# Ranking TensorE's uses of VectorE results forty places later in a two-block fp32 network on one core

## The chip, the cores and the metric

One core of a Trainium2 chip runs the whole program in one launch. The metric is device time in microseconds, from the first to the last instruction with what lies around them; lower is better.

## The reference

Two networks run one after the other on 256 tokens of width 1024, in fp32. The first has two layers: a normalised and modulated input goes through one wide projection, then through three kinds of heads, and back through `w_out`. The second has two layers on 256 latent and 256 context tokens: a projection, a convolution, a gated recurrence (mLSTM) in both directions, attention with grouped keys, three gated branches, and a convolutional feed-forward part.

```python
def _layer(x, c, ...):                       # block 1, twice
    h = _rmsnorm(x, norm_g) * (1.0 + scale) + shift
    rq, rk, rv, rg, xbc, dt_raw, z, fq, fk, fv, fg, f_raw = split(h @ w_in)
    ret = _retention(rq, rk, rv, positions) * silu(rg)
    ssd = _rmsnorm((_ssd(xs, dt, A, Bm, Cm) + d_skip * xs) * silu(z), ssd_norm_g)
    fox = _forgetting_attention(fq, fk, fv, log_f) * silu(fg)
    return x + gate * (concatenate([ret, ssd, fox]) @ w_out)

def token_mixers(hx, hc, ...):               # block 2, twice
    conv = conformer_conv(cu, ...)
    mlstm = mlstm_readout(mlstm_bidirectional(...), mo, ...)
    attn = latent_attention(q, k, v) @ w_attn_out
    return (g_conv * conv + g_mlstm * mlstm + g_attn * attn) @ w_out
```

## The kernel before, in words

Weights are streamed: `_fetch` (L486) loads a strip of up to 1024 columns, ScalarE rounds it to a high part `hi` and VectorE subtracts to get the low part `lo`. `mm3` (L529) makes each fp32 product of three matmuls (high by high, high by low, low by high), so a projection of eight row blocks is 24 matmuls, 256 columns wide (512 in block 2, layer 0, and wherever keys of both segments are made). These projections are most of TensorE's work.

Between them stand the heads. Each head is cut into pieces that wait in the queue `bg`; `strip` (L511), called by every projection, takes pieces off at a set rate before it loads its weights, and `pump` and `drain` take more by hand. A piece alternates between engines: TensorE makes scores, VectorE and ScalarE turn them into weights, TensorE transposes these (L1223, L1613) or multiplies with them (L1114, L1229, L1624). The lines that the diff touches, with what they write and read:

- L1114, `ssd_pair` (block 1): products of the decay weights `ssd_E`, into an `aux` bank.
- L1183, `ret_gate` (block 1): transpositions of the gated retention output `rope_o`.
- L1223 and L1229, `fox_pair` (block 1): transpositions of the softmax weights `ret_fox`, and products of these (`fox_pT`) with the values.
- L1521, `attn_keys` (block 2): transpositions of the rotated keys `kv`.
- L1582, `queries` (block 2): transpositions of the rotated queries `qraw`.
- L1613, in `pair`: transpositions of the scaled exponentials `tA`, of which there are two buffers; L1624, in `pv`: products of the transposed weights `pT` with the values, which become `ao`, the input of the branch projection `w_attn_out_2`.
- L1822, in `finish` (block 2): transpositions of a finished mLSTM head `h`, which become `mo`.

Other names that occur: L470, L475, L457 are helpers that issue VectorE operations, L479 issues ScalarE's; L506 is the subtraction of `_fetch`; L1671 and L1676 are the scans of the gate chain; L1101 broadcasts a row for `ssd_pair`; L1204 to L1207 make the scores of `fox_pair`, L1601 those of `pair`; L1749 and L1757 make an mLSTM head's scores and decays.

The order of the work: the program is written once, straight through, and a planner fixes the order of each engine's queue before the kernel runs. It goes through the program with its own estimates of durations; whenever an engine is free in that model, it takes, of the instructions whose inputs are ready there, the one of lowest rank. The rank is the place in the program, counted one for each instruction of any engine. `prio` (L450) adds to it for what is traced inside:

```python
    @contextmanager
    def prio(self, offset):
        self.tc.cur_priority += offset
        yield
        self.tc.cur_priority -= offset
```

Some work already uses it: the gate chain of block 2 has a rank 1000 later, background sums of the modulation 300 later. On the chip each engine then follows its queue in order, and waits where an input is late. PSUM has eight banks: three named `mm` for projections, three `aux` for heads' products, two `tr` for transpositions.

Of the kernel before, what the change touches and what calls it, by code (L numbers as in the profile page):

```python
# [18 lines left out]
P = 128  # L19
# [20 lines left out]
HAND = 320  # L40
HAND_TILES = 1
HOLD = 2

FILL_PARTS = (1, 3, 6, 9)
CTX_ROWS = (0, 4, 8, 9, 10, 11, 12, 13)
# [322 lines left out]
class Kern:  # L368
# [72 lines left out]
    def dumpx(self, name):  # L441
        if self.opts.get("dump") and name in self.opts["dump"]:
            d = self.nc.dram_tensor("dump_" + name, (P, KD, 512), F32, kind="ExternalOutput").ap()
            for k in range(KD):
                for sg in range(2):
                    if sg or self.xc:
                        self.nc.sync.dma_start(out=d[:, k, 256 * sg:256 * sg + 256], in_=self.x_view(sg)[k])

    @contextmanager
    def prio(self, offset):  # L450
# [642 lines left out]
    def ssd_pair(self, l, p, cbm, xs, xdt, yd):  # L1093
        nc = self.nc
        g = p // 4
        pr = self.ps("aux")
        prv = pr.rearrange("p (h t) -> p h t", h=2)
        E = self.bt([P, 2, 384], "ssd_E", bufs=2)
        for hh in range(2):
            h = 2 * p + hh  # L1100
            nc.tensor.matmul(prv[:, hh], self.sel(h), self.RHL, start=True, stop=True)  # L1101
            for t in range(2):
                self.ts(E[:, hh, 256 * t:256 * t + P], prv[:, hh, P * t:P * t + P], self.RT[:, t, h:h + 1], ALU.subtract,
                        0.0, ALU.min)
            self.act(E[:, hh, P:256], prv[:, hh, P:256], AF.Exp, bias=self.offb[:, h:h + 1])
        for t in range(2):
            dg = E[:, :, 256 * t:256 * t + P]
            self.act(dg, dg, AF.Exp)
        self.mul(E, E, cbm[:, g:g + 1].to_broadcast([P, 2, 384]))
        py = self.ps("aux")  # L1110
        for t, (o0, e0) in enumerate(((0, 0), (P, 256))):
            for hh in range(2):
                c0 = P * p + 64 * hh
                nc.tensor.matmul(py[64 * hh:64 * hh + 64, o0:256], xdt[:, t, c0:c0 + 64], E[:, hh, e0:e0 + 256 - o0],  # L1114
                                 start=t == 0, stop=t == 1)
        self.stt(yd[:, p], xs[:, p], self.v(f"dskip{l}", p), py[:, 0:256], ALU.mult, ALU.add)

# [51 lines left out]
    def ret_gate(self, pt, ro, rr, n, fl):  # L1169

        nc = self.nc
        gt = self.bt([P, 2, 256], "rope_o", bufs=2).rearrange("p t c -> p (t c)")
        self.act(gt, pt, AF.Tanh, scale=0.5)
        self.stt(gt, gt, 1.0, pt, ALU.add, ALU.mult)
        for t in range(2):
            for hh in range(2):
                h = 2 * n + hh
                g = gt[:, 256 * t + P * hh:256 * t + P * hh + P]
                self.stt(g, ro[:, t, P * h:P * h + P], rr[:, 4 * t + h:4 * t + h + 1], g, ALU.mult, ALU.mult)
        ptr = self.ps("tr")  # L1180
        for hh in range(2):
            for t in range(2):
                nc.tensor.transpose(ptr[:, 256 * hh + P * t:256 * hh + P * t + P],  # L1183
                                    gt[:, 256 * t + P * hh:256 * t + P * hh + P], self.ident)
        pv = ptr.rearrange("p (h t) -> p h t", h=2)
        hi, lo = fl[0][:, 2 * n:2 * n + 2], fl[1][:, 2 * n:2 * n + 2]
        self.act(hi, pv, AF.Copy, scale=0.5)
        self.stt(lo, pv, 0.5, hi.bitcast(F32), ALU.mult, ALU.subtract)

    def fox_pair(self, p, fq, fk, fv, fo):  # L1190

        nc = self.nc
        pT = self.bt([P, 2, 384], "fox_pT", bufs=2)
        for hh in range(2):
            h = 2 * p + hh
            q, k = fq[:, p, hh], fk[:, p]
            pl = self.ps("aux")
            one = self.id2[:, 32 + h:33 + h]

            e = self.bt([P, 384], "ret_fox", bufs=3)  # L1200
            for t in range(2):
                o = pl[:, P * t:P * t + P + P * t]
                w = P + P * t
                nc.tensor.matmul(o, q[:, P * t:P * t + P], k[:, 0:w], start=True, stop=False)  # L1204
                nc.tensor.matmul(o, self.nid2[:, 32 + h:33 + h].to_broadcast([P, P]), self.FHL[:, 0:w], start=False, stop=False)
                nc.tensor.matmul(o, self.FHL[:, P * t:P * t + P], one.to_broadcast([P, w]), start=False, stop=False)
                nc.tensor.matmul(o[:, P * t:], self.idr, self.fmask, start=False, stop=True)  # L1207
            sm = self.bt([P, 8], "fox_sm", bufs=2)
            for t in range(2):
                o = pl[:, P * t:P * t + P + P * t]  # L1210
                nc.vector.tensor_reduce(sm[:, t:t + 1], o, axis=AX.X, op=ALU.max)
            self.ts(sm[:, 2:4], sm[:, 0:2], -0.125, ALU.mult)
            for t in range(2):
                o = pl[:, P * t:P * t + P + P * t]
                self.act(e[:, P * t:P * t + P + P * t], o, AF.Exp, scale=0.125, bias=sm[:, 2 + t:3 + t], accum=sm[:, 4 + t:5 + t])
            nc.vector.reciprocal(sm[:, 6:8], sm[:, 4:6])
            for t in range(2):
                ev = e[:, P * t:P * t + P + P * t]
                self.act(ev, ev, AF.Copy, scale=sm[:, 6 + t:7 + t])
            ptr = self.ps("tr")  # L1220
            for b in range(3):

                nc.tensor.transpose(ptr[:, P * b:P * b + P], e[:, P * b:P * b + P], self.ident)  # L1223
            self.act(pT[:, hh], ptr[:, 0:384], AF.Copy)
        po = self.ps("aux")
        for t, (o0, e0) in enumerate(((0, 0), (P, 256))):
            for hh in range(2):
                c = slice(P * p + 64 * hh, P * p + 64 * hh + 64)
                nc.tensor.matmul(po[64 * hh:64 * hh + 64, o0:256], fv[:, t, c], pT[:, hh, e0:e0 + 256 - o0],  # L1229
                                 start=t == 0, stop=t == 1)  # L1230
        self.act(fo[:, p], po[:, 0:256], AF.Copy)

# [264 lines left out]
    def attn_keys(self, l, kvp):  # L1497

        nc = self.nc
        small = lambda n, nm: self.b2.tile([P, n], F32, tag=nm, name=f"{nm}{l}", bufs=1)  # L1500
        kv = self.s4([P, 4, 256], F32, "kv")
# [16 lines left out]
            self.rope(l, tab, kv[:, t, 0:P], t, 1, 2, r[:, 2 * t:2 * t + 2])  # L1518
        pt = self.ps("tr")
        for t in range(4):  # L1520
            nc.tensor.transpose(pt[:, P * t:P * t + P], kv[:, t, 0:P], self.ident)  # L1521

        kh, kl = [self.s4([P, 2, 512], FR, nm) for nm in ("kh", "kl")]
        for e in range(2):
# [48 lines left out]
    def attn_pieces(self, l, at, full, T0, T):  # L1573
        nc = self.nc
# [3 lines left out]
        def queries(p):  # L1578

            pt = self.ps("tr")  # L1580
            for i in range(T // P):
                nc.tensor.transpose(pt[:, P * i:P * i + P], at["q"][p // 2][:, i, P * (p % 2):P * (p % 2) + P], self.ident)  # L1582
            q = st["q"] = self.s4([P, 2, T], FR, "q")
            for e in range(2):
                src = pt[64 * e:64 * e + 64, :T]
                self.act(q[0:64, e], src, AF.Copy)
                self.sub(q[64:128, e], src, q[0:64, e].bitcast(F32))

        def pair(p, seg, t):
# [15 lines left out]
            exs = [self.t2(P * nk, "tA") for e in range(2)]  # L1605
# [3 lines left out]
            for e in range(2):  # L1609
                self.ts(exs[e], exs[e], sm[:, 6 + e:7 + e], ALU.mult)  # L1610
                pt = self.ps("tr")
                for j in range(nk):
                    nc.tensor.transpose(pt[:, P * j:P * j + P], exs[e][:, P * j:P * j + P], self.ident)  # L1613
                self.act(st["pT", e][:, :, P * t:P * t + P], pt[:, :P * nk].rearrange("p (j t) -> p j t", j=nk), AF.Copy)

        def pv(p, seg):
            nk = 2 if seg == 0 else 4
            q0 = 256 * seg - T0
            if len(at["out"]) == p:
                at["out"] += self.hl(1, "ao", T)  # L1620
            po = self.ps("aux")
            for j in range(nk):
                for e in range(2):
                    nc.tensor.matmul(po[64 * e:64 * e + 64, 0:256], at["v"][:, j, P + 64 * e:P + 64 * e + 64],  # L1624
                                     st["pT", e][:, j], start=j == 0, stop=j == nk - 1)
            hi, lo = at["out"][p]
            self.split(hi[:, q0:q0 + 256], lo[:, q0:q0 + 256], po[:, 0:256])
            at["left"] -= 1
# [96 lines left out]
    def head_pieces(self, l, hd, head, T0, T, mo):  # L1725
        nc = self.nc
        q, k = head["q"], head["k"]
# [84 lines left out]
        def finish():  # L1812
# [6 lines left out]
            for f in range(2):  # L1819
                pt = self.ps("tr")[:, :T]  # L1820
                for i in range(ni):
                    nc.tensor.transpose(pt[:, P * i:P * i + P], ho[:, i, P * f:P * f + P], self.ident)  # L1822
                (hi, lo), = self.hl(1, "mo", T)
                w = self.v(f"m_norm2{l}", 2 * hd + f)
                self.act(hi, pt, AF.Copy, scale=w)
# [187 lines left out]
```

## Time and profile before

| | |
|---|---|
| median of 3 runs | 2198.2 us (2197.14 to 2200.11) |
| profiled execution, its own time | 2200.12 us |
| its span | 2198.4 us |
| mean granted TensorE clock | 0.997 |
| busy: TensorE, weight loads, VectorE, ScalarE | 2146.0, 1910.5, 1714.4, 1000.6 us |
| instructions | 38207, of them 14481 matmuls |
| DMA | 330.71 MB, mean 150 GB/s |

PE is TensorE's matmuls, PEld its weight loads, DVE is VectorE, ACT ScalarE, POOL GpSimd, SP the engine that issues the loads. A row `PE tr L1613 <- DVE tA L470` tells that TensorE, about to write a `tr` bank from line 1613, stood idle until VectorE had written `tA` in line 470. An fp32 matmul outside `mm3` and outside a transposition is recorded as two matmuls. A matmul's end is modelled, and the next one often starts before it.

### The profile page before, as it was taken

What the parts mean: (1) busy time and instruction counts of PE and PEld (TensorE: products, weight loads), DVE (VectorE), ACT (ScalarE), POOL (GpSimd) and SP (SyncE); (2) the same over time, 40 slices, a digit from 0 to 9 for tenths busy, and PEclk for the clock granted to TensorE, in tenths of its full rate; (3) what the DMA queues carried; (4) which work ended last, traced back from release to release, by engine and by line L of the source; (5) the groups of instructions that cost most, each with busy time, mean ns of one, the idle gap of its engine ahead of it and who ended that gap; (6) DMA issues with size and microseconds to landing.
All of it is one profiled execution on the core that took longest, in us unless ns stands there. A gap on an engine that the chain in (4) does not pass through costs nothing. (4 is left out here: it accounts for less than half of the span.)

```text
span 2198.4 us, 38207 instructions
## 1 busy us (share of the span) xinstructions
PE 2146.0 (98%) x14481; PEld 1910.5 (87%) x14481; DVE 1714.4 (78%) x3551; ACT 1000.6 (46%) x1828; POOL 72.0 (3%) x657
## 2 busy tenths in 40 slices
PE   6999999999999999999999999999999999999999
PEld 5999989898877888888888888888887999999999
DVE  6986889798975999775476777766689977567877
ACT  4656555555455333432333443323355434445654
POOL 0000000001000000000000000000000000000000
PEclk9999999999999999999999999999999999999999
DMA  8665746567321144235443244453432453674665
GB/s 301 198 202 176 268 135 201 160 215 235 106 68 53 50 128 144 82 123 160 125 154 110 82 125 128 122 181 122 122 116 72 128 156 126 210 249 145 186 195 158
DMA packets 98264, 330.71 MB, mean 150 GB/s; under 512 B 10912, under 2 KB 14368, under 8 KB 97952
## 3 DMA queue, kind: packets, MB, share of 16 engines
q1 hardware_dynamic: 97632, 326.47, 47.0%
q8 instruction: 114, 1.87, 0.4%
q0 software_dynamic: 448, 1.81, 0.2%
q14 instruction: 70, 0.57, 0.1%
HBM read 325.08 MB, written 3.15 MB: 149 GB/s over the span
## 5 line engine op out<-in xcount | busy, mean ns | idle before, releaser
L479 ACT ACTIVATE hi<-raw 128x1024 fp32r<-128x1024 f32 (+3 forms) x494 | 492.0, 997 | 709.0 <-PE mm L534 440.0
L506 DVE TENSOR_TENSOR lo<-raw,hi 128x1024 fp32r<-128x1024 f32 (+3 forms) x494 | 565.0, 1144 | 231.0 <-ACT hi L479 228.3
L533 PE MATMUL mm<-h,hi 128*128 128x512 f32 (+1 forms) x1296 | 445.7, 345 | 3.4 <-ACT th L479 1.2
L535 PE MATMUL mm<-h,lo 128*128 128x512 f32 (+1 forms) x1296 | 442.0, 342 | 2.5 <-DVE lo L506 2.5
L534 PE MATMUL mm<-h,hi 128*128 128x512 f32 (+1 forms) x1296 | 442.1, 342 | 0.4 <-DVE h L475 0.4
L533 PEld LDWEIGHTS mm<-h,hi 128*128 128x128 f32 x1296 | 244.3, 189 | 33.7 <-ACT h L479 1.5
L535 PEld LDWEIGHTS mm<-h,lo 128*128 128x128 f32 x1296 | 244.8, 189 | 32.3 <-DVE lo L506 3.3
L534 PEld LDWEIGHTS mm<-h,hi 128*128 128x128 f32 x1296 | 244.7, 189 | 30.3 <-DVE h L475 0.8
L533 PE MATMUL mm<-hi,h 128*128 128x256 f32 x608 | 173.2, 285 | 0.8 <-ACT h L479 0.7
L534 PE MATMUL mm<-lo,h 128*128 128x256 f32 x608 | 171.8, 283 | 1.2 <-DVE lo L506 1.2
L535 PE MATMUL mm<-hi,h 128*128 128x256 f32 x608 | 172.2, 283 | 0.1
L533 PE MATMUL mm<-h_hi,hi 128*128 128x256 f32 x512 | 143.7, 282 | 4.0 <-ACT h_hi L479 2.3
L535 PE MATMUL mm<-h_hi,lo 128*128 128x256 f32 x512 | 143.4, 282 | 1.3 <-DVE lo L506 1.2
L534 PE MATMUL mm<-h_lo,hi 128*128 128x256 f32 x512 | 143.8, 282 | 0.7 <-DVE h_lo L457 0.5
L475 DVE SCALAR_TENSOR_TENSOR cv<-glu,vec,cv 128x512 f32<-128x512 f32 (+1 forms) x240 | 136.4, 615 | 2.5 <-ACT cv L479 2.4
L766 DVE SCALAR_TENSOR_TENSOR ada<-ada,cb 128x1024 f32<-128x1024 f32 x104 | 126.8, 1220 | 1.3 <-DMA ada<-aall 0.8
L533 PEld LDWEIGHTS mm<-hi,h 128*128 128x128 f32 x608 | 114.4, 188 | 2.7 <-ACT h L479 1.8
L534 PEld LDWEIGHTS mm<-lo,h 128*128 128x128 f32 x608 | 114.5, 188 | 2.1 <-DVE lo L506 1.4
L535 PEld LDWEIGHTS mm<-hi,h 128*128 128x128 f32 x608 | 114.6, 189 | 1.3 <-DVE h L475 0.9
L533 PEld LDWEIGHTS mm<-h_hi,hi 128*128 128x128 f32 x512 | 96.1, 188 | 5.1 <-ACT h_hi L479 2.7
L535 PEld LDWEIGHTS mm<-h_hi,lo 128*128 128x128 f32 x512 | 96.1, 188 | 2.1 <-DVE lo L506 1.9
L534 PEld LDWEIGHTS mm<-h_lo,hi 128*128 128x128 f32 x512 | 96.3, 188 | 1.6 <-DVE h_lo L457 1.1
(679 smaller groups left out, 4821.9 us busy)
## 6 DMA issues: line engine op xcount, KB each, us to landing
raw<-wall SPq DMA_DIRECT2D x400, 512.0 KB, 3.7
ada<-aall SPq DMA_DIRECT2D x120, 512.0 KB, 4.2
raw<-wall SPq DMA_DIRECT2D x32, 384.0 KB, 3.1
raw<-wall SPq DMA_DIRECT2D x32, 320.0 KB, 3.1
raw<-wall SPq DMA_DIRECT2D x32, 256.0 KB, 2.7
yd<-aall SPq DMA_DIRECT2D x2, 1024.0 KB, 10.3
qk_ret<-aall SPq DMA_DIRECT2D x2, 1024.0 KB, 11.3
xs<-aall SPq DMA_DIRECT2D x2, 1024.0 KB, 10.8
```

The lines of the kernel that those rows point to most:

```text
L475: return self.nc.vector.scalar_tensor_tensor(out=out, in0=a, scalar=s, in1=b, op0=op0, op1=op1)
L479: return self.nc.scalar.activation(out, a, f, bias=bias, scale=scale, **kw)
L506: self.last_lo = self.nc.vector.tensor_tensor(lo[:, :w], raw[:, :w], hi[:, :w].bitcast(F32), op=ALU.subtract)
L533: mm(ps, ah, bh, start=first and n == 0, stop=False)
L534: mm(ps, ah, bl, start=False, stop=False)
L535: self.last_mm = mm(ps, al, bh, start=False, stop=last and n == len(A) - 1)
L766: nc.vector.scalar_tensor_tensor(out=out, in0=raw, scalar=1.0, in1=self.cb[which][i], op0=ALU.mult, op1=ALU.mult, accum_out=m[:, n:n + 1])
```

## The change

Two helpers are added, `late_t` for a transposition and `late_mm` for a product; each traces its instruction with a rank 40 higher. Nine lines call them in place of the direct call. Nothing else changes: the instructions, their operands and their buffers are the same, and so are the ranks of all others.

```diff
+T_LATE = 40
...
+    def late_t(self, out, a):
+
+        with self.prio(T_LATE):
+            self.nc.tensor.transpose(out, a, self.ident)
+
+    def late_mm(self, *a, **kw):
+        with self.prio(T_LATE):
+            self.nc.tensor.matmul(*a, **kw)
...
@@ ssd_pair
-                nc.tensor.matmul(py[64 * hh:64 * hh + 64, o0:256], xdt[:, t, c0:c0 + 64], E[:, hh, e0:e0 + 256 - o0],
+                self.late_mm(py[64 * hh:64 * hh + 64, o0:256], xdt[:, t, c0:c0 + 64], E[:, hh, e0:e0 + 256 - o0],
                                  start=t == 0, stop=t == 1)
@@ ret_gate
-                nc.tensor.transpose(ptr[:, 256 * hh + P * t:256 * hh + P * t + P],
-                                    gt[:, 256 * t + P * hh:256 * t + P * hh + P], self.ident)
+                self.late_t(ptr[:, 256 * hh + P * t:256 * hh + P * t + P], gt[:, 256 * t + P * hh:256 * t + P * hh + P])
@@ fox_pair
-                nc.tensor.transpose(ptr[:, P * b:P * b + P], e[:, P * b:P * b + P], self.ident)
+                self.late_t(ptr[:, P * b:P * b + P], e[:, P * b:P * b + P])
...
-                nc.tensor.matmul(po[64 * hh:64 * hh + 64, o0:256], fv[:, t, c], pT[:, hh, e0:e0 + 256 - o0],
+                self.late_mm(po[64 * hh:64 * hh + 64, o0:256], fv[:, t, c], pT[:, hh, e0:e0 + 256 - o0],
                                  start=t == 0, stop=t == 1)
@@ attn_keys
-            nc.tensor.transpose(pt[:, P * t:P * t + P], kv[:, t, 0:P], self.ident)
+            self.late_t(pt[:, P * t:P * t + P], kv[:, t, 0:P])
@@ queries
-                nc.tensor.transpose(pt[:, P * i:P * i + P], at["q"][p // 2][:, i, P * (p % 2):P * (p % 2) + P], self.ident)
+                self.late_t(pt[:, P * i:P * i + P], at["q"][p // 2][:, i, P * (p % 2):P * (p % 2) + P])
@@ pair
-                    nc.tensor.transpose(pt[:, P * j:P * j + P], exs[e][:, P * j:P * j + P], self.ident)
+                    self.late_t(pt[:, P * j:P * j + P], exs[e][:, P * j:P * j + P])
@@ pv
-                    nc.tensor.matmul(po[64 * e:64 * e + 64, 0:256], at["v"][:, j, P + 64 * e:P + 64 * e + 64],
+                    self.late_mm(po[64 * e:64 * e + 64, 0:256], at["v"][:, j, P + 64 * e:P + 64 * e + 64],
                                      st["pT", e][:, j], start=j == 0, stop=j == nk - 1)
@@ finish
-                    nc.tensor.transpose(pt[:, P * i:P * i + P], ho[:, i, P * f:P * f + P], self.ident)
+                    self.late_t(pt[:, P * i:P * i + P], ho[:, i, P * f:P * f + P])
```

## Rows read from the trace of the kernel before

**Rows 1.** The page: busy time and share of an engine; TensorE's granted clock in 40 slices.

```profile
PE 2146.0 (98%) x14481; PEld 1910.5 (87%) x14481; DVE 1714.4 (78%) x3551; ACT 1000.6 (46%) x1828; POOL 72.0 (3%) x657
...
PEclk9999999999999999999999999999999999999999
```

**Rows 2.** Who TensorE waited for: total us, times, longest us.

```profile
PE tr L1613 <- DVE tA L470: 3.1, 4, 2.0
...
PE tr L1822 <- DVE h L475: 1.9, 3, 0.8
PE tr L1521 <- DVE kv L457: 1.8, 2, 1.0
...
PE tr L1223 <- ACT ret_fox L479: 0.9, 3, 0.5
...
PE aux L1114 <- DVE ssd_E L457: 0.6, 1, 0.6
...
PE tr L1183 <- DVE rope_o L475: 0.5, 1, 0.5
PE aux L1229 <- ACT fox_pT L479: 0.5, 2, 0.3
...
PE tr L1582 <- DVE qraw L457: 0.4, 1, 0.4
```

**Rows 3.** TensorE's timeline, block 2 layer 1: start us, us shown; idle time in brackets.

```profile
1857.58 0.28 PE L534 MATMUL mm<-h,hi 128*128 128x256 f32 x1
1857.70 0.28 PE L535 MATMUL mm<-h,lo 128*128 128x256 f32 x1
1858.81 0.44 PE L1822 MATMUL tr<-cst,h 128*128 128x128 f32 x2 [0.83 <-DVE h L475]
1859.01 0.36 PE L533 MATMUL mm<-h,hi 128*128 128x256 f32 x1
```

**Rows 4.** TensorE's timeline at the longest wait of L1613.

```profile
1680.93 1.06 PE L1613 MATMUL tr<-cst,tA 128*128 128x128 f32 x8 [1.96 <-DVE tA L470]
```

**Rows 5.** VectorE's timeline ahead of that wait.

```profile
1675.70 1.20 DVE L1671 TENSOR_TENSOR_SCAN gate<-ones,gate 32x512 f32<-32x512 f32 x1
...
1680.30 0.88 DVE L470 TENSOR_SCALAR tA<-tA,at_sm 128x512 f32<-128x512 f32 x2
```

**Rows 6.** Windows, 12 us: busy time and count of each engine, clock, DMA share, GB/s.

```profile
1676.00:1688.00 12.00, 10.04 (x48) 6.34 (x47) 9.29 (x16) 4.61 (x12) 0.63 (x7) 0.86 0.17 44
```

**Rows 7.** TensorE's timeline at the first query transpositions, block 2 layer 0.

```profile
594.01 0.40 PE L534 MATMUL mm<-h,hi 128*128 128x512 f32 x1
...
594.47 0.40 PE L533 MATMUL mm<-h,hi 128*128 128x512 f32 x1
595.29 0.33 PE L1582 MATMUL tr<-cst,qraw 128*128 128x128 f32 x1 [0.43 <-DVE qraw L457]
```

**Rows 8.** TensorE's timeline in the fox pairs, block 1 layer 0.

```profile
158.98 0.87 PE L1229 MATMUL aux<-fox_pT,fox_v 128*64 128x256 f32 x6 [0.29 <-ACT fox_pT L479]
159.78 0.70 PE L1204 MATMUL aux<-fox_k,qk_fox 128*128 128x256 f32 x2
...
161.93 0.34 PE L535 MATMUL mm<-hi,h_lo 128*128 128x256 f32 x1
```

**Rows 9.** Around the last attention products, layer 0: TensorE's and VectorE's timeline; readers of ao.

```profile
712.38 1.98 PE L1749 MATMUL aux<-q,k 128*128 128x512 f32 x4
...
716.56 0.59 PE L1749 MATMUL aux<-q,k 128*128 128x256 f32 x2
...
713.80 0.42 DVE L457 TENSOR_TENSOR ao<-aux,ao 128x256 fp32r<-128x256 f32 x1
...
L533 PE MATMUL mm<-ao,hi x8: 392/397/583, 742.0 to 757.0; 128*128 128x512 f32 x8
```

**Rows 10.** TensorE's timeline at the last head's transpositions, layer 1.

```profile
1941.00 0.44 PE L1822 MATMUL tr<-cst,h 128*128 128x128 f32 x2 [0.67 <-DVE h L475]
```

**Rows 11.** Who GpSimd's queue waited for.

```profile
POOL tA L1268 <- PE tr L1613: 82.2, 44, 8.6
```

## The prediction

> **What bounds the kernel now.** The page comes first: TensorE (PE) shows matmuls in 98% of a span of 2198.4 us, and the granted clock stays at full speed in nearly every slice [rows 1]. So only two things can move the time: the idle time left on TensorE, and the order in which its queue is laid out. The second view is the list of who TensorE waits for. Eight of its rows belong to lines that the diff touches [rows 2]; they add up to 3.1 + 1.9 + 1.8 + 0.9 + 0.6 + 0.5 + 0.5 + 0.4 = 9.7 us in 17 waits. That column counts from the modelled end of the product before, though. In an undisturbed run of 256-column products one starts 0.12 us after the last while each is shown 0.28 us long [rows 3]: a wait hides another 0.28 - 0.12 = 0.16 us under that end. With it the 17 waits cost 9.7 + 17 x 0.16 = 12.4 us. The Trainium skill, Perfetto Trace Analysis, section Identifying the Most-Contended Engine, says that matmul busy share is a poor measure, since matmuls are pipelined: by the idle column alone the change could give back 9.7 us at most; the starts of the rows above side with the page and make it 12.4.
>
> The third view is the timeline at the longest of them. The last transposition of an attention pair in block 2, layer 1 stands idle for 1.96 us [rows 4], because VectorE runs the gate chain's scans and their neighbours from 1675.70 on, before the scaling that the transposition needs starts at 1680.30 [rows 5]. In the 12 us around it the mean granted clock is 0.86 [rows 6]: 0.14 x 12 / 0.5 = 3.4 us at 1.2 in place of 2.4 GHz, after the wait. At half speed that costs at most 1.7 us more.
>
> **What the change does, by place.** Nothing is added or removed: the same instructions run, no DMA moves, and no semaphore gets another producer. Nine kinds of work on TensorE get a rank 40 higher. A rank is the place in the program, one per instruction of any engine, so a moved instruction falls behind only such ready work as stands less than 40 places after it. The count decides, and can be made from the code. Take the first query transpositions of layer 0 [rows 7]. Behind the four of them, at places 0 to 3, the program has a memset and four copies (to 8), the first attention pair with 22 instructions (9 to 30) and the load, rounding and subtraction of the next strip (31 to 33). The projection's first product is place 34. Four products have run when the transposition waits, so the product right behind it is place 38: products 38 and 39 now go ahead of rank 40, and two products of this width take 0.46 us, as from 594.01 to 594.47.
>
> I counted so at every place where a touched line runs in the trace.
> - **Attention transpositions (L1613).** There are 24 groups, and the product right behind them is 101 to 378 places on: TensorE is several projections ahead of the attention. Forty places pass nothing. The 3.1 us stay, among them the 1.96 us and the slow clock.
> - **Key transpositions (L1521).** Products 87 to 140 places on. The 1.8 us stay.
> - **Fox transpositions (L1223).** Products 132 to 340 places on; only in some groups do parts of the next scores (9 to 14 on) go first. The 0.9 us stay.
> - **SSD products (L1114).** Products over 119 on. In half of the 16 groups one broadcast of the next pair (5 on) goes first; the 0.6 us wait is in the other half, and stays.
> - **Fox value products (L1229).** In 8 groups the next pair's scores, 5 to 31 on, go first: up to 12 instructions, 159.78 to 161.93, or 2.15 us [rows 8]. That covers the 0.29 us wait: 0.29 + 0.16 = 0.45 us back. The other wait (0.2 us) has products 79 on and stays.
> - **Retention gate (L1183).** The wait of 0.5 us has its next product exactly 40 places on, a tie. I take nothing; the bounds are 0 and 0.66.
> - **Queries (L1582).** The two products counted above cover 0.46 of the 0.43 + 0.16 us: 0.46 us back.
> - **Attention value products (L1624).** They pass 1 to 4 of the next scores, and after the last group in layer 0 the score and decay products of head 0 go first, from 712.38 to 716.56, 4.2 us [rows 9]. What waits for that output is the branch projection: VectorE ends it at 714.2 and TensorE first reads it at 742.0 [rows 9], so 27.8 us cover it. I cost it at nothing; without that cover it would be 4.2 us.
> - **Head results (L1822).** The wait of 0.83 us in layer 1 has products 33 to 39 places on: seven products x 0.12 = 0.84 us go first [rows 3], and 0.84 of the 0.83 + 0.16 us come back. The wait of 0.67 us has its next product at 40, a tie again [rows 10]: 0, or 0.67 + 0.16 = 0.83. The third, 0.35 us, has products 85 on.
>
> Where a planner breaks a tie, no row shows. An equal rank leaves the older work first in the simplest queue, so I take zero and keep 0.66 + 0.83 = 1.5 us for the range.
>
> **The sum:** 0.45 + 0.46 + 0.84 = 1.75 us; with some hidden starts at places without an idle entry I take 2 us. The profiled execution took 2200.1 us around its span of 2198.4; it becomes 2198.1. The median shown is 2198.2, 1.9 lower, so the forecast there is 2196.2. A median of this kernel is told apart from no change from about 0.2% on, 4.4 us.
>
> What hangs on the count is smaller than what hangs on its echo. The planner picks from what is ready, so a moved group shifts its later choices, from the first SSD pair (90 us) on. Whether they fall back into the old order I can't read off the trace; that is what the wider cases are for.
>
> **The rivals.**
> A. *The title comes true:* all 17 waits go, with the slow clock: 12.4 + 1.7 = 14.1 us, 2184.1. For it: the waits are there, and each is of the kind named. Against: 24 + 2 + most of 16 groups have nothing within forty places. Chance 0.10.
> B. *The echo takes the long wait away:* if VectorE's order changes by one scan near 1680, 1.96 + 0.16 + 1.7 = 3.8 us go beside the 2: 2192.4. For it: that wait depends on a row of fillers just ahead of one scaling, while the groups of the other pairs wait 0.2 us or less. Against: nothing in layer 1's attention is itself passed. Chance 0.14.
> C. *The echo brings such waits (slower):* the place is the attention of block 2, where scans, strip subtractions (1.2 us each) and scalings share VectorE's queue. Each pair before whose scaling the planner puts two or more fillers costs 3.8 us by the same rows. From two more on it decides: 2198.2 + 7.6 - 2 = 2203.8. For it: VectorE is busy in 78% of the span and there are 24 pairs. Against: one pair of 24 has it now. Chance 0.11.
> D. *Buffers are held longer (slower):* the two buffers of scaled exponentials come free only when the transpositions have run; the next owner's memset waits for that 44 times, 82.2 us in all [rows 11]. If the 12 pairs of layer 0 slipped by over 27.8 / 12 = 2.3 us each, the branch projection would wait; at the 24 products of a projection, 24 x 0.23 = 5.5 us each, it would be 38 us, 2234. The Trainium skill, Perfetto Trace Analysis, section Optimization Strategy, reads a gap that repeats as a sign of too few buffers, and asks to make the dependency itself sooner, not its reader later. Against: the waits here end with VectorE's result, and nothing passes these groups. Chance 0.03.
> E. *Nothing at all:* order and time as before, 2198.2. Chance 0.05.
>
> **The numbers.** The forecast has 0.57; with ties and a little echo it spans 2193.8 to 2198.5. Faster by over 0.2% (under 2193.8) are A and B: 0.24. Slower by over 0.2% (over 2202.6) are C and D: 0.14. Within 0.2% are the forecast and E: 0.62. The range takes in the forecast, E, B and the lower half of C, and leaves out A, D and the rest of C, about 0.19 of the chance: 2191 to 2203.5.
>
> **What would show it.** Right: L1613, L1521 and L1223 keep their waits within some tenths; the 0.83 us wait of L1822 and the 0.43 us of L1582 are gone; the value products of the fox pairs stand behind the next scores; busy time of all engines is unchanged. Wrong, by A: the eight rows fall under 3 us together, so that ready work within forty places existed which the order of before doesn't show. Wrong, by B or C: the sum changes through L1613 alone, with another number of slow-clock stretches. By D: the branch projection's first product waits for VectorE.

## The result and the profile after

Against the kernel before, timed beside it (median 2198.75 us of 4 runs), the changed kernel takes 2212.07 us (2211.13 to 2212.94, 4 runs): a ratio of 1.0061, with a 95% interval of 1.0043 to 1.0078. It is 13.3 us slower, outside the range given. The profiled execution has a span of 2209.3 us.

The page, busy time first, then the granted clock:

```profile
PE 2160.3 (98%) x14481; PEld 1911.9 (87%) x14481; DVE 1715.0 (78%) x3551; ACT 1001.6 (45%) x1828; POOL 71.6 (3%) x657
...
PEclk8999999999999999999999999999999999999999
```

Beside [rows 1] VectorE and ScalarE are as they were. TensorE is busy 14.3 us longer with the same 14481 matmuls, and the time in which it is not (span less busy) fell from 52.4 to 49.0 us. So in sum TensorE waits less, and the same work takes more time: 14.3 - 3.4 = 10.9 us more in the span of these two executions (2198.4 to 2209.3). Who TensorE waited for (line 454 is the new transposition, 458 the new product; other line numbers are some ten higher than before):

```profile
PE tr L454 <- DVE tA L481: 3.1, 5, 2.0
...
PE tr L454 <- DVE kv L468: 2.0, 2, 1.0
...
PE tr L454 <- ACT ret_fox L490: 1.1, 4, 0.5
...
PE tr L454 <- DVE h L486: 0.9, 2, 0.5
...
PE aux L458 <- DVE ssd_E L468: 0.6, 1, 0.6
...
PE tr L454 <- DVE rope_o L486: 0.4, 1, 0.4
...
PE aux L458 <- ACT fox_pT L490: 0.4, 1, 0.4
```

These answer [rows 2]: 8.5 us where there were 9.7. The queries' wait is gone, the head results' fell from 1.9 to 0.9 us, and the long attention wait stands as it was, 1.97 us. The waits say nearly what was forecast; the loss stands in TensorE's timeline. First, the SSD group of [rows 2]'s line 1114, before and after:

```profile
90.39 0.87 PE L1114 MATMUL aux<-ssd_E,xdt 128*64 128x256 f32 x8
91.19 0.38 PE L1101 MATMUL aux<-RHL,id 128*128 128x256 f32 x1
91.41 0.28 PE L535 MATMUL mm<-h_hi,lo 128*128 128x256 f32 x1
```

```profile
91.51 0.65 PE L458 MATMUL aux<-ssd_E,xdt 128*64 128x256 f32 x2
92.09 0.38 PE L1112 MATMUL aux<-RHL,id 128*128 128x256 f32 x1
92.40 0.86 PE L458 MATMUL aux<-ssd_E,xdt 128*64 128x256 f32 x6
93.20 0.38 PE L546 MATMUL mm<-h_hi,lo 128*128 128x256 f32 x1
```

The four products (eight records, from one start to the next work 0.80 us) and the broadcast behind them took 1.02 us. Now the broadcast stands behind the first product: 0.58 + 0.31 + 0.80 = 1.69 us, so 0.67 us more. That happens in 8 of the 16 groups: 5.4 us. Second, the third pair of attention in layer 0, before and after:

```profile
683.05 2.28 PE L1624 MATMUL aux<-pT,kv 128*64 128x256 f32 x16
685.26 0.33 PE L1582 MATMUL tr<-cst,qraw 128*128 128x128 f32 x1
```

```profile
688.88 0.39 PE L544 MATMUL mm<-h,hi 128*128 128x512 f32 x1
689.11 0.40 PE L545 MATMUL mm<-h,hi 128*128 128x512 f32 x1
...
689.66 0.65 PE L458 MATMUL aux<-pT,kv 128*64 128x256 f32 x2
690.24 0.49 PE L544 MATMUL mm<-h,hi 128*128 128x512 f32 x1
690.67 0.65 PE L458 MATMUL aux<-pT,kv 128*64 128x256 f32 x2
691.24 0.50 PE L545 MATMUL mm<-h,hi 128*128 128x512 f32 x1
...
695.68 0.65 PE L458 MATMUL aux<-pT,kv 128*64 128x256 f32 x4
696.26 0.44 PE L454 MATMUL tr<-cst,qraw 128*128 128x128 f32 x2
```

Eight products took 2.21 us in one piece. Now six of them alternate one by one with the projection's products. From 689.66 to 696.26 are 6.60 us; less six projection products at their undisturbed 0.235 us (688.88 to 689.11, to 689.35), 5.19 us: 2.98 us more. Third, two groups of four are laid out so with the next pair's scores, as here (before, then after):

```profile
612.53 1.16 PE L1624 MATMUL aux<-pT,kv 128*64 128x256 f32 x8
613.62 0.50 PE L1601 MATMUL aux<-kh,q 128*128 128x512 f32 x1
...
614.64 0.39 PE L533 MATMUL mm<-h,hi 128*128 128x512 f32 x1
```

```profile
617.79 0.65 PE L458 MATMUL aux<-pT,kv 128*64 128x256 f32 x2
618.37 0.50 PE L1611 MATMUL aux<-kh,q 128*128 128x512 f32 x1
...
621.60 0.50 PE L544 MATMUL mm<-h,hi 128*128 128x512 f32 x1
```

Four products and four scores: 2.11 us, then 3.81 us; 1.7 us more, twice. Two other groups of four lost their first product to the far side of the scores (649.29 to 652.00 against 642.26 to 644.38: 0.6 us each), and the last group of eight 0.3 us. In all 5.4 + 3.0 + 3.4 + 1.2 + 0.3 = 13.3 us.

That the medians also lie 13.3 us apart is chance: the span of these two executions grew by 10.9 us. Another 1.1 us was lost ahead of the first SSD group, where no touched line runs (it starts at 91.51 in place of 90.39 us; the granted clock of the first 46 us was 0.85 in place of 1.00, part of them at 1.2 in place of 2.4 GHz). Some 1.5 us came back behind the long attention wait, where the clock was 0.86 before [rows 6] and is 1.00 now (1690 to 1702 us). The other 2 us are the waits that went, and other stretches at a lower clock.

A product that shows 128*64 in the rows is half-width: it uses 64 columns of weights in place of 128 and writes 64 of the 128 partitions, the lower or the upper half. Call a run of half-width products with nothing between them an island. Counted in the traces, SSD, fox and attention had 16 + 16 + 18 = 50; now 24 + 16 + 33 = 73. So each new one costs 14.3 / 23 = 0.62 us by busy time, 13.3 / 23 = 0.58 by the steps above.

### The profile page after: what moved, and what is told of

It reads as the page before. It is cut to its first block, busy times and chain, and to the rows that moved or that the text cites. A ratio compares the mean times of both kernels' runs of the same rounds, so it can differ in the third digit from the quotient of the medians.

```text
span 2209.3 us, 38212 instructions
## 1 busy us (share of the span) xinstructions
PE 2160.3 (98%) x14481; PEld 1911.9 (87%) x14481; DVE 1715.0 (78%) x3551; ACT 1001.6 (45%) x1828; POOL 71.6 (3%) x657
## 3 DMA queue, kind: packets, MB, share of 16 engines
q8 instruction: 114, 1.87, 0.3%
## 6 DMA issues: line engine op xcount, KB each, us to landing
xs<-aall SPq DMA_DIRECT2D x2, 1024.0 KB, 10.9
```

## The experiments

The theory, islands (each cut of a group costs TensorE time), stands against two rivals: lateness (results come later and their readers slip) and echo (the whole order shifts). Times are medians of 5 to 11 runs beside 21 to 24 of the kernel before (2199.05, in the last four 2198.95 us).

**One kind of product put back.**

```diff
-                self.late_mm(py[64 * hh:64 * hh + 64, o0:256], xdt[:, t, c0:c0 + 64], E[:, hh, e0:e0 + 256 - o0],
+                nc.tensor.matmul(py[64 * hh:64 * hh + 64, o0:256], xdt[:, t, c0:c0 + 64], E[:, hh, e0:e0 + 256 - o0],
```

> As the changed kernel, but the SSD products keep their old rank. Theory (islands): the loss is TensorE step time, not waits. A later rank lets other work in between the products of one group, and every island of products that is made costs: a lone product steps 0.576 us to its successor, four in a row 0.80 us (SSD) or 1.09 us (attention). The changed kernel has 23 more islands than the one before (SSD 16 to 24, attention 18 to 33) and 14.3 us more step time: 0.62 us each. Here the SSD groups are whole again, 8 islands fewer: 8 x 0.62 = 5.0 us under the changed kernel's 2212.1, 2207.1 us; the SSD products' steps fall from 17.4 to 12.8 us, the attention products' stay at 28.9. Rival (lateness): what costs is that results come later and their readers slip; the SSD products go at most one broadcast later, 0.3 us with no wait behind it, so 2211 to 2213 us. Rival (echo): the whole order shifts and the time may go anywhere; then the loss does not follow the SSD stages (63 to 154 us, 337 to 400 us), and attention changes too.

Measured: 2206.37 us, ratio 1.0035 (1.0023 to 1.0048), 65 islands. The steps of the SSD products fell from 17.4 to 12.8 us, those of attention stayed. Lateness misses, and the loss follows the SSD products, as echo says it should not.

**Only the transpositions; only the products.** The first calls `nc.tensor.matmul` in all three places; the second has `self.prio(0)` in `late_t`.

> As the changed kernel, but all three kinds of products keep their old rank; only the transpositions go forty later. Islands: 50 islands of half-width products, as before the change, so the whole 14.3 us of step time goes; the waits that fell (1.3 us for the head results, 0.6 for the queries) stay gone: 2196 to 2199 us. Lateness: the transpositions are most of what is moved and sit ahead of every chain, so at least half of the 13.3 us stays: 2205 us or more. Echo: anything between 2196 and 2212, with waits in other lines.

> The other half: only the products go forty later, the transpositions keep their rank. Islands: SSD 24, attention 37, fox 16 as ever: 27 more than before the change, 27 x 0.62 = 16.7 us, and the waits of the transpositions come back: 2213 to 2217 us, slower than the whole change. Lateness: under half of the loss, 2199 to 2205 us. Echo: no figure; not above 2212 more often than below.

Measured: 2197.95 us, 0.9996 (0.9987 to 1.0005), and 2214.51 us, 1.0073 (1.0061 to 1.0086). The whole loss hangs on the products. The transpositions alone make no difference that can be told from none: idle time down by 3.3 us, busy time up by 2.4 (2148.4). Of that, some 1.7 us arose ahead of the first SSD group (it starts at 92.11 in place of 90.39 us), before any touched line, at a granted clock of 0.83 from 30 to 40 us.

**As late, but in one piece.** `self.head` is the product before; it is set to None where a group begins.

```diff
-        with self.prio(T_LATE):
-            self.nc.tensor.matmul(*a, **kw)
+        with self.prio(-4000 if self.head else T_LATE), self.tc.issue_after(self.head.ins) if self.head else nullcontext():
+            self.head = self.nc.tensor.matmul(*a, **kw)
```

> All ranks forty later as in the changed kernel, but behind the first product of a group the other products are ranked ahead of everything and may not pass it, so a group stays in one piece at its late place. Islands: SSD 16, fox 16, attention 17, 1 fewer than before the change: 2195 to 2199 us. Lateness: the place is as late as in the changed kernel, so 2209 to 2213 us. Echo: between.

Measured: 2197.58 us, 0.9995 (0.9986 to 1.0004), 49 islands. The groups start as late as in the changed kernel and the loss is gone, so lateness falls: what costs is the cuts and not the place.

**What a cut costs: the end of a run, or the neighbour?** In the SSD and attention groups the two loops over halves and row blocks change places, so that the lower half's products all come first.

> The kernel before, no rank changed; in the SSD and attention groups all products of the first half of the partitions come ahead of those of the second half, where before they took turns. This asks what a lone product loses: the end of an island, or the neighbour in the other half that runs beside it. Islands stay (SSD 16, fox 16) or fall (attention 18 to 12). If only the ends of islands cost: 6 x 0.62 = 3.7 us gained, 2195 us. If the neighbour counts: a half-width product in turn takes 0.28 us (1.09 us for four), a full-width one of the same 256 columns 2 x 0.216 = 0.43 us (scores q,k), so one without a neighbour should take about 0.43: the SSD groups 1.1 in place of 0.80 us (16 x 0.3 = 4.8), attention groups of eight 3.0 in place of 2.21 (8 x 0.8 = 6.4), of four 1.3 in place of 1.09 (0.8 in all): 12 - 3.7 = 8 us more, 2207 us.

Measured: 2202.11 us, 1.0011 (1.0002 to 1.0020), between the two forecasts. The timeline, an SSD group and an attention group of eight:

```profile
90.19 0.88 PE L1114 MATMUL aux<-ssd_E,xdt 128*64 128x256 f32 x8
91.00 0.39 PE L1101 MATMUL aux<-RHL,id 128*128 128x256 f32 x1
...
654.34 2.86 PE L1624 MATMUL aux<-pT,kv 128*64 128x256 f32 x16
657.13 0.66 PE L1582 MATMUL tr<-cst,qraw 128*128 128x128 f32 x4
```

The group of eight grew from 2.21 to 2.79 us, as a lost neighbour says (3.0). The SSD group stays at 0.81, and the attention groups of four at 1.10; those estimates were wrong: two products of one half, then two of the other, still run side by side. In the group of eight, by the starts of its single records, the first product of the upper half comes 0.92 us after the first of the lower, when two of its four have gone.

**The same cut at full width.** These two kernels tell whether any fp32 group pays for a cut. They don't compute what the reference does: the SSD products write all 128 partitions and leave out the sum over the two row blocks.

```diff
-                self.late_mm(py[64 * hh:64 * hh + 64, o0:256], xdt[:, t, c0:c0 + 64], E[:, hh, e0:e0 + 256 - o0],
-                                 start=t == 0, stop=t == 1)
+                self.late_mm(py[:, o0:256], xdt[:, t, P * p:P * p + P], E[:, hh, e0:e0 + 256 - o0],
+                                 start=True, stop=True)
```

> Together with the run of full-width groups kept whole. As the changed kernel, but each SSD product is full width (128 columns of xdt in place of 64, over all 128 partitions, with no accumulation over the two row blocks), which is not the reference's computation. The SSD groups are split as in the changed kernel, 24 islands. If a split costs because products lose the neighbour in the other half, a full-width product has none to lose: this kernel and the whole one differ by under 2 us. If every end of an fp32 group costs, they differ by 8 x 0.57 to 0.62 = 4.6 to 5 us. Both should be above their half-width kin by about 16 x 0.5 us = 8 us (group 1.30 in place of 0.80 us): this one 2220 us or, with nothing lost by the split, 2215 us.

> The full-width SSD products again (not the reference's computation: 128 columns of xdt, no accumulation), with the SSD groups at their old rank and so whole, 16 islands. 2206.4 us of the half-width kernel with whole SSD groups + 16 x 0.5 us = 2214 to 2215 us by both theories; what tells them apart is the distance to the split one, under 2 us or 4.6 to 5 us.

Measured: split 2214.40 us, 1.0070 (1.0056 to 1.0084); whole 2217.54 us, 1.0078 (1.0066 to 1.0091). The first group of each, split and whole:

```profile
92.00 0.70 PE L458 MATMUL aux<-ssd_E,xdt 128*128 128x256 f32 x2
92.34 0.47 PE L1112 MATMUL aux<-RHL,id 128*128 128x256 f32 x1
92.65 1.04 PE L458 MATMUL aux<-ssd_E,xdt 128*128 128x256 f32 x6
93.44 0.36 PE L546 MATMUL mm<-h_hi,lo 128*128 128x256 f32 x1
```

```profile
91.98 1.57 PE L1125 MATMUL aux<-ssd_E,xdt 128*128 128x256 f32 x8
93.31 0.36 PE L1112 MATMUL aux<-RHL,id 128*128 128x256 f32 x1
93.51 0.28 PE L546 MATMUL mm<-h_hi,lo 128*128 128x256 f32 x1
```

With the broadcast, whole 1.33 + 0.20 = 1.53 us, split 0.34 + 0.31 + 0.79 = 1.44. At full width a cut costs nothing: the split kernel should have been slower by under 2 us, or by 4.6 to 5. Its median is 3.1 us lower; the intervals overlap, and why it isn't the same was not tried. A whole group takes 1.33 in place of 0.80 us: that is what the neighbour saves.

**Ranks that coincide.** All products of a group get the rank of the first.

```diff
-        with self.prio(T_LATE):
-            self.nc.tensor.matmul(*a, **kw)
+        with self.prio(T_LATE - self.nth):
+            self.nc.tensor.matmul(*a, **kw); self.nth += 1
```

> The changed kernel, but all products of a group get one rank (that of the first, forty later) in place of ranks that count up. Theory (zip): the counted-up ranks of a moved group fall on the same numbers as the projection's or the next scores', and the two are laid one by one, as in the six lone products from 689.42 to 694.43 us of the changed kernel, 1.00 us a round. With one rank they can't be zipped with what stands behind; what becomes ready in the middle of a group with a lower rank still splits it. Islands: SSD 24, fox 16, attention 26 in place of 33: 7 fewer than in the changed kernel, 7 x 0.62 = 4.3 us: 2207.8 us, with no six lone products in layer 0's third pair. If ties of rank have no part in it: 2211 to 2213 us.

Measured: 2208.17 us, 1.0041 (1.0029 to 1.0054). (The times in this expectation count from 0.25 us later than the rows.) The third pair now:

```profile
689.40 0.65 PE L458 MATMUL aux<-pT,kv 128*64 128x256 f32 x2
689.97 0.50 PE L544 MATMUL mm<-h,hi 128*128 128x512 f32 x1
690.40 1.94 PE L458 MATMUL aux<-pT,kv 128*64 128x256 f32 x14
692.27 0.50 PE L545 MATMUL mm<-h,hi 128*128 128x512 f32 x1
```

One cut is left instead of six, and 2.87 - 0.24 = 2.63 us in place of 5.19. This alternation was made by the ranks. In the two groups of four that alternate with scores, two cuts are left of three.

**Versions that beat both.** Each group starts with the half whose weights come last (`for hh in (1, 0)` for fox, `for e in (1, 0)` for attention), and the rest follows it as in the run in one piece; the rank of the first is the old one.

> Nothing later: transpositions and the first product of each group have the rank of the kernel before. Each group starts with the half whose weights come last, and its other products are ranked ahead of everything and behind the first, so all groups are in one piece: SSD 16, fox 8 (16 before the change), attention 12 (18). Islands: 14 fewer than before the change, 14 x 0.62 = 8.7 us: 2190.4 us, faster than both. Rival (lateness): the early product of a fox pair used time that it now takes later, and the groups end later: 2198 to 2202 us.

Measured: 2195.32 us, 0.9982 (0.9973 to 0.9990): faster than before the change, but by less than half of what was expected. TensorE's busy time fell by 8.9 us (2137.1), as priced, but its idle time grew from 52.4 to 55.2 us: 6.1 us less in the span, 3.7 in the medians (the profiled execution lies 1.3 us under its median, that of the kernel before 1.1 us over). The next three runs are about the waits: the same with the transpositions late; with the fox transpositions left alone; with the fox products left as before.

> All groups in one piece as in the run with old ranks (36 islands, 2195.3 us measured), and the transpositions forty later as in the run with transpositions alone. That run had gained 8.9 us of TensorE steps against the kernel before, as 14 x 0.62 says, but idle time in front of the fox transpositions grew from 0.9 to 3.5 us and in all by 3 us. If those waits are of the kind that later transpositions cover (head results 1.9 to 0.9 us, queries 0.6 us, part of the 3.5), this is 2 to 4 us faster again: 2191 to 2193 us. If later transpositions only trade one wait for another: 2195 us, as with old ranks.

> As the run with all groups joined and the transpositions later, but the fox transpositions keep their old rank. It asks whether the waits of 3.5 us in front of them come from their rank. If so: 1 to 2.5 us slower than with all transpositions later, 2193 to 2195 us. If they come from the joining (the lone early product that filled the wait is gone): the same within 1 us.

> As the run with all groups joined and the transpositions later, but the fox products as in the kernel before: one lone product, then three, 44 islands. By the slots alone the fox pairs are 8 x (0.576 + 0.795 - 0.80) = 4.6 us slower than joined. If the joined fox pairs give back 2.6 us in waits for their transpositions, as the run with old ranks shows, this one is 2 us slower than that with all joined; if they give back all, it is equal or faster. 2193 to 2195 us.

Measured: 2193.65 us, 0.9974 (0.9963 to 0.9984); 2194.40, 0.9978 (0.9969 to 0.9987); 2195.47, 0.9984 (0.9975 to 0.9992). All three beat the kernel before, by up to 5.3 us. The first two can't be told apart (0.75 us); the first was expected at 2191 to 2193 us. The waits in front of the fox transpositions, in this order:

```profile
PE tr L454 <- ACT ret_fox L490: 4.2, 7, 1.5
```

```profile
PE tr L1233 <- ACT ret_fox L490: 4.9, 7, 2.2
```

```profile
PE tr L454 <- ACT ret_fox L490: 1.1, 4, 0.5
```

Their rank has little part in it (4.2 against 4.9); joining the fox products makes them (1.1 without). That fits a lone early product that filled a wait. So the 4.6 us of steps saved there bring 2195.47 - 2193.65 = 1.8 us.

| islands | kernel | us | TensorE busy |
|---|---|---|---|
| 36 | joined, late transpositions | 2193.65 | 2134.4 |
| 36 | joined, late transpositions but for fox | 2194.40 | 2139.0 |
| 36 | joined, old ranks | 2195.32 | 2137.1 |
| 44 | joined but for fox, late transpositions | 2195.47 | 2143.1 |
| 44 | halves apart | 2202.11 | 2148.5 |
| 49 | late, in one piece | 2197.58 | 2148.1 |
| 50 | before | 2199.05 | 2146.0 |
| 50 | transpositions only | 2197.95 | 2148.4 |
| 65 | without SSD | 2206.37 | 2152.6 |
| 66 | one rank | 2208.17 | 2157.2 |
| 73 | the change | 2212.07 | 2160.3 |
| 77 | products only | 2214.51 | 2163.9 |

From 50 islands up the time follows the count: (2214.51 - 2199.05) / 27 = 0.57 us each. Below 50 it follows less well, as the fox pairs show, and not at all with the halves apart: what counts is the neighbour, and islands count it only where the halves take turns. The busy times are those of one execution each, and good to about 2 us: the first SSD group, 719 matmuls in, starts anywhere from 90.2 to 92.3 us, later where the clock granted in the first 50 us was lower.

## Why the prediction was wrong

**The step that failed** is the price of a passed product. "Attention value products ... They pass 1 to 4 of the next scores ... I cost it at nothing", and for the SSD products "In half of the 16 groups one broadcast of the next pair (5 on) goes first". Most counts were good: 8 of 16 SSD groups, the scores, no transposition of attention; the six projection products that the third pair passes were not counted. But the broadcast goes between the first product and the second, and the scores go between the products one by one. Work that goes first was taken as an exchange of places that costs TensorE nothing ("busy time of all engines is unchanged"). With half-width products it isn't: TensorE's busy time grew by 14.3 us, about 0.6 us for each of 23 cuts.

**What a cut costs.** The two halves of the partitions run side by side. Three products in the changed kernel, and eight in the joined one with old ranks:

```profile
650.99 1.08 PE L458 MATMUL aux<-pT,kv 128*64 128x256 f32 x6
652.00 0.50 PE L546 MATMUL mm<-h,lo 128*128 128x512 f32 x1
```

```profile
653.45 1.95 PE L458 MATMUL aux<-pT,kv 128*64 128x256 f32 x16
655.33 0.38 PE L1611 MATMUL aux<-kh,q 128*128 128x256 f32 x1
```

From the start of a run to the next work, one product takes 0.58 us, two take 0.58 as well (695.68 to 696.26 above), three 1.01, seven 1.87 (690.40 to 692.27 above), eight 1.88. So each pair costs 0.43 us, a product left without its neighbour 0.43 as well, and a run 0.15 around it: 0.43 + 0.15 = 0.58, 2 x 0.43 + 0.15 = 1.01, 4 x 0.43 + 0.15 = 1.87. A product cut from its neighbour adds 0.58, and the work that it is cut by takes longer too: the broadcast 0.31 in place of 0.22 us, a projection product of the third pair 0.43 in place of 0.235. The full-width runs lost no neighbour and paid nothing: there too the broadcast took 0.31, but the lone product only 0.34. The Trainium skill, TensorEngine Tiling (Array Packing), section Tiling Modes, says that tiles work independently of each other, and that a change of tiling mode, unlike a change of tile, drains TensorE. The 0.43 us of a pair agrees with the first. The 0.15 us around each run would fit the second, but no run here shows that it, or a part of it, is a drain.

**Why the products were cut.** A group moved by a constant keeps ranks that count up by one, and forty places on they meet the ranks of unmoved work that count up by one too. By the count in the code, the third pair's products have ranks 7060 on, and the projection beside them 7060 on: each tie goes to the older product, then comes one of the other. In the two alternating groups of four it is the same: products from 6529 and from 6945 on, scores from 6528 and from 6944 on. The prediction met ties twice, and took them as a question of who goes first. The run with one rank shows what they did. For SSD there is no tie: the broadcast now has the lower rank and goes in behind the first product (why not ahead of it, no run shows); so that run left those eight cuts.

**What held.** The 3.1 us of L1613 stayed, the 1.96 us wait with them, and L1521 and L1223 kept theirs within 0.2 us; the 0.83 us of L1822 and the 0.43 us of L1582 went. Alone, the transpositions gave 1.1 us (by the interval between a gain of 2.9 and a loss of 1.1); the forecast for them was 2 us less the 0.45 of the fox value products. Taking ties as "the older work first" was right: the tied waits of L1183 and L1822 still cost 0.37 and 0.55 us.

**What else did not hold.** The 0.45 us of the fox value products did not come: they stand behind the next scores as forecast, but the first pair now waits 0.36 us in place of 0.29. The wait that went is the other one, which was to stay. The slow clock was counted with the 1.96 us wait, and the changed kernel's profile has the wait without it. And the range ends at 2203.5, below rival C's own 2203.8, so it took in no part of C.

**The rivals.** A, B, D and E did not come. C had only the sign, by luck: it expected longer waits for VectorE, and TensorE's waits became shorter. The prediction argued that TensorE is the bound, and then had no rival in which TensorE's own work grows.

## What to carry to other kernels

Where an engine is busy 98% of the span, ask of a new order first what it does to the work of that engine, then to its waits: count the runs of products that share the array in halves, and price every cut (here 0.6 us). A group that has to be late should move as one piece, its first product late and the rest tied to it. Moving a group by a constant rank can lay it one by one into whatever stands at those ranks, as three attention groups show.

## What the runs showed of the hardware

- Two half-width fp32 products of 256 columns in different halves take 0.43 us together, as long as one alone; at full width a group of four (two of 256 columns, two of 128) took 1.22 to 1.38 us, where 2 x 0.43 + 2 x 0.215 is 1.29.
- They need not be neighbours in the queue: in the order two lower, two upper, the SSD group still took 0.81 us; with four and four, half of the overlap was lost (2.79 us, against 1.88 with all of it and, as an estimate, 8 x 0.43 + 0.15 = 3.59 with none).
- A group of eight whose two halves start together took 1.88 us; with the upper half's first product 0.34 us behind, it took 2.21, and with the first product gone ahead 0.58 + 1.87. Started with the half whose attention weights are ready last, 7 of the 8 groups of eight took 1.88.
